# HGRN2's diagonal 32-position blocks as 32-column products, four column tiles to a product, into a compact tile

## The chip, the cores and the metric
One core of a Trainium2 chip runs the whole program. The metric is the device time of one execution in microseconds; a run's time stands as it was measured, and the profile is one further look at one execution, taken by the hardware profiler.

## The reference, cut to what matters
One inference step of a decoder layer: an input projection, two groups of four heads each (mLSTM and HGRN2), an output projection, and a SwiGLU feed-forward, for 1024 prompt tokens and 8 decode sequences of 4 tokens. The change is in HGRN2 alone, whose chunk is

```python
b = jnp.cumsum(lf, axis=2)
inter = jnp.einsum('bhtk,bhkv->bhtv', q * jnp.exp(b), S)
dec = jnp.exp(jnp.where(mask[:, :, None], b[:, :, :, None, :] - b[:, :, None, :, :], -jnp.inf))
A = jnp.einsum('bhtk,bhsk,bhtsk->bhts', q, k, dec)
o = inter + jnp.einsum('bhts,bhsv->bhtv', A, v)
```

The matrix A (position s, position t, with s not after t) has a decay for each feature between s and t. It must be right for every pair of positions in a chunk; how it is put together is free.

## The kernel before, in words
**Layout and stages.** Features lie on the 128 partitions, tokens along the free axis. The tokens come in three blocks of 288, 384 and 384 (the first holds 256 prompt tokens and the 32 decode tokens), that is 2, 3 and 3 chunks of 128 positions. First the input projection runs: 33 weight tiles, for each head four units per block (`unit`, L121, and `emit_k`, L124). A unit is one weight tile times one block: eight steps of three matmuls, the weights and the tokens being split into a high and a low part (L135, L136, L137). Then follow the output projection and the feed-forward, all in matmuls of 264 columns.

**What sets the order.** Every engine runs its instructions in the order in which the program emits them. Projection matmuls are emitted unit by unit; after every six of them `hook` (L63) is called, which gives each open generator a turn. `mix_b(h, b)` (L745) is such a generator, one for each head and block of HGRN2, twelve in all. `yield 2` means: go on at the second hook from here, so twelve projection matmuls lie between two parts. Weight splits (`split`, L86: ScalarE copies the high part, GpSimd subtracts) and the decode sequences (`sample_core`, L600) are generators too.

**How A is put together.** `mix_b` doubles a distance `lv` from 1 to 64. At each level it multiplies the keys with the queries on TensorE (`prod`, L754), then scales every second group of `lv` queries on VectorE (L801), the other groups of keys on GpSimd (L802), and makes the next level's gate products on VectorE (L806). The next product needs both. From each level's product only the entries belong to A in which s lies in an even group of `lv` positions and t in the odd group behind it; the diagonal comes from a product ahead of the levels. For the diagonal and levels 1 to 16 `prod` multiplies all 128 positions of a chunk with all 128 (L757), although only the four 32x32 blocks on the diagonal are read. The first block has, for the diagonal and levels 1 and 2, a further 32x32 product for the decode tokens (L759), which goes to the tile `PB`.

**From PSUM into the square tile `AT`** ([128, 3 chunks, 128]): for each of the four 32-row blocks one VectorE instruction. The diagonal is a product with the identity (L772), levels 1 to 8 are masked copies (L813, masks `mk`), level 16 is a plain copy of 16 rows (L821). Levels 32 and 64 have smaller products (L788: two column tiles of 32; L793) and are copied by ScalarE (L825, L827). Then keys and values are transposed (L840, L843), the state is brought forward (L857, L867), and `AT` and the state are multiplied with the values and queries (L877, L879).

Of the kernel before, what the change touches and what calls it, by code (L numbers as in the profile page):

```python
# [9 lines left out]
F32 = mybir.dt.float32  # L10
# [24 lines left out]
LEVELS = [1, 2, 4, 8]  # L35
# [5 lines left out]
def hybrid_step(ctx: ExitStack, tc: tile.TileContext, i, o):  # L41
# [109 lines left out]
    cst = mp.tile([128, 232], F32, name="cst")  # L151
    msk = mp.tile([128, 64], U8, name="msk")
# [28 lines left out]
    mk = {1: msk[:, 0:16], 2: msk[:, 16:32], 4: msk[:, 32:48], 8: msk[:, 48:64]}  # L181
# [16 lines left out]
    def norm_rstd(key, n, acc, w=(2, 3)):  # L198
        """the rstd of n tokens on all partitions, from the squares summed over the feature tiles in acc"""
        yield w[0]  # L200
        pc = bank()
        parts = [(t, min(128, n - 128 * t)) for t in range(3)]
        rs = cn.tile([128, 4], F32, tag="nrs", name="nrs", bufs=2)
        if parts[2][1] < 128:
            nc.vector.memset(rs, 1.0)
        for t, c in parts:
            nc.tensor.matmul(pc[:c, t:t + 1], acc[:, 128 * t:128 * t + c], ones, start=True, stop=True)
        for c, t0, t1 in [(128, 0, 3)] if n == 384 else [(128, 0, 2), (n - 256, 2, 3)]:
            nc.vector.tensor_scalar(rs[:c, t0:t1], pc[:c, t0:t1], 1.0 / D, EPS, op0=OP.mult, op1=OP.add)
        nc.gpsimd.tensor_tensor(rs[:, 0:3], rs[:, 0:3], mhalf[:, 0:3], op=OP.pow)  # L210
        done.add(("rs", key))
        yield w[1]
        pb = bank()
        for t, c in parts:
            nc.tensor.transpose(pb[:, 128 * t:128 * t + c], rs[:c, t:t + 1].to_broadcast([c, 128]), ident[:c, :c])
        return pb

    def norm_gen(key, x, hv, lv, acc, vg, w=(2, 3), pb=None, lo_dve=(0, 4), step=2):
        """x = hv + lv = x * rstd * g, rstd from the squares summed over the feature tiles in acc"""
        n = x.shape[2]  # L220
        if pb is None:
            pb = yield from norm_rstd(key, n, acc, w)

        def low(m):
            (nc.vector if m in lo_dve else nc.gpsimd).tensor_tensor(lv[:, m, :], x[:, m, :], hv[:, m, :].bitcast(F32),
                                                                    op=OP.subtract)
        for m in range(KT):
            nc.vector.scalar_tensor_tensor(x[:, m, :], x[:, m, :], col(vg + m), pb[:, :n], op0=OP.mult, op1=OP.mult)
            nc.scalar.activation(hv[:, m, :], x[:, m, :], AF.Copy)
            if m:  # L230
                low(m - 1)
            if m == KT - 1:
                low(m)
            if (m + 1) % step == 0:
                yield 1

    # ------------------------------------------------------------------ token mixers
# [3 lines left out]
    # per-feature constants  # L241
# [7 lines left out]
    def conv_consts():  # L249
        # half the convolution and half the output gate: y sigmoid(y) = (y/2) (tanh(y/2) + 1)  # L250
# [17 lines left out]
    # ---- mLSTM gates  # L268
# [84 lines left out]
    def gates_sample(ig, lf):  # L353
# [36 lines left out]
        for a in ATs:  # L390
            nc.gpsimd.memset(a, 0.0)
# [4 lines left out]
    # ---- mLSTM  # L396
# [93 lines left out]
    def norm_cols(s, sqs, nch, d2=None, p=128):  # L490
        """s = (sqs / 128 + EPS * d2) ** -0.5"""
# [108 lines left out]
    def sample_core(h_off, w, vnorm, st_in, decay, out_state, n_io, d2, k_scale, later=None):  # L600
        """the decode sequences of one head group: four heads x 32 tokens on the partitions"""
# [126 lines left out]
    # ---- HGRN2  # L728
    ATs = [mp.tile([128, 3, 128], F32, name=f"AT{j}") for j in range(2)]
    atn = [0]  # L730
# [14 lines left out]
    def mix_b(h, b):  # L745
        ncb, npr, n = NCH[b], NPR[b], BL[b]
        q, f, k = S["qb", h, b], S["f", h, b], S["kb", h, b]
        AT = ATs[atn[0] % 2]
# [5 lines left out]
        def prod(ps, a, c_, lo=0):  # L754
            for c in range(ncb):
                s = slice(c * 128, c * 128 + 128)
                nc.tensor.matmul(ps[:, s], a[:, s], c_[:, s], start=True, stop=True)  # L757
            if lo:
                nc.tensor.matmul(ps[32 * h:32 * h + 32, 256:288], a[:, 256:288], c_[:, 256:288], start=True, stop=True,  # L759
                                 tile_position=(0, 32 * h))  # L760

        def quads(fn):
            for j in range(4):
                fn(slice(32 * j, 32 * j + 32))
# [4 lines left out]
        prod(ps, k, q, samp)  # L769

        def dg(js):
            nc.vector.tensor_tensor(AT[js, :ncb, js], ps[js, :npr].rearrange("p (c t) -> p c t", t=128)[:, :, js],  # L772
                                    ident[js, None, js].to_broadcast([32, ncb, 32]), op=OP.mult)
        quads(dg)
        if samp:
            nc.vector.tensor_tensor(PB[hs, hs], ps[hs, 256:288], ident[hs, hs], op=OP.mult)
        yield 2
        G, go, lv = f, 0, 1
        while lv < 128:
# [3 lines left out]
            if lv <= 16:  # L783
                prod(ps, k, qp, sm)
# [23 lines left out]
            if lv <= 8:  # L808
                def ext(js):
                    src = pc[js, :, js].rearrange("p c (n two l) -> p c n two l", two=2, l=lv)[:, :, :, 1, :]  # L810
                    dst = AT[js, :ncb, js].rearrange("p c (n two l) -> p c n two l", two=2, l=lv)[:, :, :, 1, :]
                    m = mk[lv][js].rearrange("p (n l) -> p n l", l=lv)
                    nc.vector.copy_predicated(dst, m[:, None].to_broadcast([32, ncb, 16 // lv, lv]), src)  # L813
                quads(ext)
                if sm:
                    src = ps[hs, 256:288].rearrange("p (n two l) -> p n two l", two=2, l=lv)[:, :, 1, :]
                    dst = PB[hs, hs].rearrange("p (n two l) -> p n two l", two=2, l=lv)[:, :, 1, :]
                    nc.vector.copy_predicated(dst, mk[lv][hs].rearrange("p (n l) -> p n l", l=lv), src)
            elif lv == 16:
                for j in range(4):  # L820
                    nc.vector.tensor_copy(AT[32 * j:32 * j + 16, :ncb, 32 * j + 16:32 * j + 32],  # L821
                                          pc[32 * j:32 * j + 16, :, 32 * j + 16:32 * j + 32])
# [80 lines left out]
    # ------------------------------------------------------------------ unit list  # L903
# [37 lines left out]
    # output projection; the token order from here on: 1024 prompt tokens, 32 decode tokens  # L941
# [62 lines left out]
    # feed-forward, first NPLAIN feature tiles  # L1004
# [36 lines left out]
    # feed-forward, the other feature tiles: pairs of them (rows of A) times two halves of the tokens (columns of B), the  # L1041
    # contraction in two halves: the seven products of Strassen and Winograd
# [21 lines left out]
    def t_prep():  # L1064
        """T1 = B12 - B11, T2 = B22 - T1, T3 = B22 - B12, T4 = B21 - T2"""
# [71 lines left out]
    def gsplit(g, u, dve=False):  # L1137
        """the factors of the products: A11 A12 | S1 = A21 + A22, S2 = S1 - A11 | S3 = A11 - A21, A22 | S4 = A12 - S2"""
# [52 lines left out]
    def g_out(u, r, th, j, ps, other=None, op=None):  # L1191
        """row tile r, token half th, columns j: ps or ps + other is there"""
# [54 lines left out]
    # down projection: NS times four feature tiles in the same way (the contraction in two pairs of tiles, pairs of output  # L1247
    # tiles, halves of the tokens), the last two tiles plainly
# [3 lines left out]
    def memb(r):  # L1252
        """place r of the ring of operands: hi and lo of two feature tiles, half of the tokens"""
# [18 lines left out]
    def raw_ff(c, f):  # L1272
        """the two column blocks of a feature tile: halves of the tokens, in the last chunk halves of each half"""
# [16 lines left out]
    def stage1(c):  # L1290
        """B11, T1 = B12 - B11, T2 = B22 - T1, B21"""
# [26 lines left out]
    def diffs(c, k):  # L1318
        """T3 = B22 - B12, T4 = B21 - B11 - T3"""
# [7 lines left out]
    def stage2(c):  # L1327
        """B22, T3, T4"""
# [28 lines left out]
    def dsplit(g):  # L1357
        """A11 A12 A22 | S1 = A21 + A22, S2 = S1 - A11, S4 = A12 - S2, S3 = A11 - A21"""
# [5 lines left out]
        def pair(j):  # L1364
            # the weights of the last chunk stay: five tiles in the ring, three in free places of the other ring
# [49 lines left out]
    def d_step(g, p):  # L1415
        """a product for a pair of output tiles, halves of the tokens; in the last chunk for two pairs, the quarters of a half"""
# [27 lines left out]
    # the first NPLAIN feature tiles of the down projection plainly  # L1444
# [36 lines left out]
    # the final norm: the first half of the tokens, then two quarters  # L1481
    fac, frs = {}, {}

    def xs(m, q):
        """tile m for a half of the tokens (q = 0, 1) or quarter q = 2, 3"""
        return x2[0][:, m, 528 * q:528 * q + 528] if q < 2 else x2[0][:, m, q * QN:(q + 1) * QN]

    def fsquare(m, q, acc=None):
        """the squares of a tile, in a sum's first tile or for facc"""
# [5 lines left out]
    def facc(acc, sq, dve, wait=0):  # L1495
        """a generator: acc += sq"""
# [8 lines left out]
    def squares(h):  # L1505
        """the first four tiles, half h of the tokens"""
# [14 lines left out]
    def last_squares(m, q):  # L1521
        """the last four tiles of a quarter, as they are done"""
# [48 lines left out]
    def final_half():  # L1571
        """the first half of the tokens"""
# [20 lines left out]
    # ------------------------------------------------------------------ emission  # L1593
# [14 lines left out]
    nc.scalar.dma_start(cst, i["cst"][:, 128:360])  # L1608
# [62 lines left out]
    nc.vector.tensor_copy(msk, cst[:, 168:232])  # L1671
# [165 lines left out]
def _constants():  # L1837
    p = np.arange(128)
    cst = np.zeros((128, 360), np.float32)
# [5 lines left out]
    msk = cst[:, 296:360]  # L1845
    r = p % 32
    for j, l in enumerate(LEVELS):
        n = np.arange(16) // l
        msk[:, 16 * j:16 * j + 16] = ((r[:, None] // (2 * l)) == n[None, :]) & ((r[:, None] % (2 * l)) < l)
    return cst  # L1850
# [63 lines left out]
```

## Time and profile before

| | |
|---|---|
| three runs | 1456.2, 1456.57, 1451.91 us (median 1456.2) |
| profiled execution | span 1451.2 us; the page gives no other time of its own |
| TensorE | 1376.6 us busy (95%), 10384 matmuls |
| VectorE | 904.0 us (62%), 2120 instructions |
| ScalarE | 528.8 us (36%) |
| GpSimd | 731.9 us (50%) |
| mean granted TensorE clock | 0.980 |

The span runs from the first to the last instruction of one execution. PE is TensorE's matmul, PEld its weight load, DVE is VectorE, ACT ScalarE, POOL GpSimd, SP SyncE. A line such as L757 is a line of the kernel. Matmul records overlap: one lasts longer than the distance to the next, so the time that a matmul takes from the stream is read from starts.

### The profile page before, as it was taken

The numbers are of one execution on the slowest core, as the hardware profiler recorded it, in microseconds if no ns is written. First come the engines' busy times: TensorE is split into PE (matmuls) and PEld (weight loads), VectorE is DVE, ScalarE is ACT, GpSimd is POOL, SyncE is SP. The second block draws the span as 40 slices with busy tenths as digits, with TensorE's granted clock in tenths as the row PEclk, the third lists the DMA queues.
The fourth block names the chain that finished last, engine by engine and source line by source line (L and its number), as shares of the span: only waits on it lengthen the run. The fifth ranks groups of instructions, "written<-read, shape, count | busy, mean of one in ns | idle before, by whom it ended". The sixth has DMA issues, their size and how long they took to land. (4 is left out here: it accounts for less than half of the span.)

```text
span 1451.2 us, 26916 instructions
## 1 busy us (share of the span) xinstructions
PE 1376.6 (95%) x10384; PEld 1339.6 (92%) x10384; DVE 904.0 (62%) x2120; ACT 528.8 (36%) x1195; POOL 731.9 (50%) x720
## 2 busy tenths in 40 slices
PE   7879999999999999999989999999999999998886
PEld 7769999999999998899989999999999998888885
DVE  7876657666776767745472233233322389999986
ACT  6554433322222223223344343333334423333343
POOL 5313213234343435223456655656555778888854
PEclk9989999999999999999999999999999999999998
DMA  6012212320010114443542222222212563334303
GB/s 216 22 42 76 64 37 86 109 79 29 33 44 18 44 32 133 142 148 119 182 139 74 82 89 89 69 72 89 89 64 69 182 235 134 134 134 145 123 30 121
DMA packets 85833, 138.54 MB, mean 95 GB/s; under 512 B 8240, under 2 KB 61000, under 8 KB 85192
## 3 DMA queue, kind: packets, MB, share of 16 engines
q1 hardware_dynamic: 85272, 136.57, 28.7%
q8 instruction: 82, 1.34, 0.4%
q14 instruction: 47, 0.39, 0.1%
q10 hardware_dynamic: 432, 0.24, 0.1%
HBM read 107.03 MB, written 29.75 MB: 94 GB/s over the span
## 5 line engine op out<-in xcount | busy, mean ns | idle before, releaser
L135 PE MATMUL mm<-HI,whi 128*128 128x384 f32 (+2 forms) x1160 | 382.7, 330 | 6.9 <-ACT gA L302 2.9
L137 PE MATMUL mm<-HI,wlo 128*128 128x384 f32 (+2 forms) x1160 | 363.8, 314 | 1.3 <-POOL wlo L97 1.3
L136 PE MATMUL mm<-LO,whi 128*128 128x384 f32 (+2 forms) x1160 | 363.9, 314 | 0.7 <-DVE LO L961 0.4
L135 PEld LDWEIGHTS mm<-HI,whi 128*128 128x128 f32 x1160 | 222.2, 192 | 12.2 <-ACT gA L302 3.2
L136 PEld LDWEIGHTS mm<-LO,whi 128*128 128x128 f32 x1160 | 222.4, 192 | 1.7 <-DVE LO L961 0.6
L137 PEld LDWEIGHTS mm<-HI,wlo 128*128 128x128 f32 x1160 | 221.9, 191 | 1.8 <-POOL wlo L97 1.8
L97 POOL TENSOR_TENSOR wlo<-raw,whi 128x512 fp32r<-128x512 f32 x90 | 119.7, 1339 | 144.1 <-ACT whi L96 99.2
L1158 POOL TENSOR_TENSOR wlo<-S,whi 128x512 fp32r<-128x512 f32 x78 | 107.0, 1373 | 87.1 <-ACT whi L1157 85.8
L1229 PE MATMUL mx<-T,whi 128*128 128x264 f32 x640 | 118.2, 284 | 0.0
L1229 PEld LDWEIGHTS mx<-T,whi 128*128 128x128 f32 x640 | 99.0, 188 | 0.0
L802 POOL TENSOR_TENSOR ck<-ck,wib 128x192 f32<-128x192 f32 (+2 forms) x72 | 41.2, 572 | 100.6 <-PE mx L757 56.2
L1229 PE MATMUL mx<-HI,whi 128*128 128x264 f32 x320 | 91.0, 284 | 0.0
L1229 PE MATMUL mx<-T,wlo 128*128 128x264 f32 x320 | 90.9, 284 | 0.0
L1229 PE MATMUL mx<-HI,wlo 128*128 128x264 f32 x320 | 90.9, 284 | 0.0
L1229 PE MATMUL mx<-LO,whi 128*128 128x264 f32 x320 | 90.7, 283 | 0.0
L1282 POOL TENSOR_TENSOR LO<-rg,HI 128x528 fp32r<-128x528 f32 x52 | 78.4, 1514 | 10.5 <-ACT HI L1281 5.8
L1435 PE MATMUL mx<-HI,whi 128*128 128x264 f32 x208 | 62.3, 300 | 9.9 <-DVE X L1439 9.9
L1157 ACT ACTIVATE whi<-S 128x512 fp32r<-128x512 f32 x80 | 50.2, 629 | 58.4 <-DVE S L1146 58.4
L1229 PE MATMUL mm<-HI,wlo 128*128 128x264 f32 x240 | 68.2, 284 | 0.0
L1229 PE MATMUL mm<-HI,whi 128*128 128x264 f32 x240 | 68.2, 284 | 0.0
L1229 PE MATMUL mm<-LO,whi 128*128 128x264 f32 x240 | 67.9, 283 | 0.0
L1439 DVE TENSOR_TENSOR X<-X,mx 128x264 f32<-128x264 f32 x160 | 60.7, 418 | 8.2 <-PE mx L1435 8.2
(544 smaller groups left out, 3751.8 us busy)
## 6 DMA issues: line engine op xcount, KB each, us to landing
rg<-d_ff SPq DMA_DIRECT2D x42, 528.0 KB
raw<-in_wA SPq DMA_DIRECT2D x31, 512.0 KB
raw<-in_wgu SPq DMA_DIRECT2D x24, 512.0 KB
raw<-in_wd SPq DMA_DIRECT2D x22, 512.0 KB
d_ff<-sg SPq DMA_DIRECT2D x40, 264.0 KB
rg<-in_wgu SPq DMA_DIRECT2D x20, 512.0 KB
d_h<-X SPq DMA_DIRECT2D x4, 1056.0 KB
X<-d_x SPq DMA_DIRECT2D x4, 1056.0 KB
```

The costliest lines, as they stand in the source:

```text
L97: (nc.gpsimd if pool else nc.vector).tensor_tensor(lo[:, s], raw[:, s], hi[:, s].bitcast(F32), op=OP.subtract)
L135: nc.tensor.matmul(ps[:, :n], wh, rh[:, k, :], start=(k == 0), stop=False)
L136: nc.tensor.matmul(ps[:, :n], wh, rl[:, k, :], start=False, stop=False)
L137: nc.tensor.matmul(ps[:, :n], wl, rh[:, k, :], start=False, stop=(k == nk - 1))
L802: nc.gpsimd.tensor_tensor(ke, ke, gv[:, :, 1:2].to_broadcast([128, nb, lv]), op=OP.mult)
L1157: nc.scalar.activation(hi[:, s], t, AF.Copy)
L1158: (nc.vector if dve else nc.gpsimd).tensor_tensor(lo[:, s], t, hi[:, s].bitcast(F32), op=OP.subtract)
L1229: nc.tensor.matmul(ps[:, :QN], a[:, w], b_[:, kk, c], start=new and kk == 0 and x == 0, stop=kk == 3 and x == 2, skip_group_check=True)
L1282: (nc.vector if dve else nc.gpsimd).tensor_tensor(lw, src, h.bitcast(F32), op=OP.subtract)
L1435: nc.tensor.matmul(ps[:, :QN], a[:, w], b_[k][:, cs], start=new and k == 0 and x == 0, stop=k == 1 and x == 2, skip_group_check=True)
L1439: nc.vector.tensor_tensor(y, y, ps[:, :QN], op=OP.add)
```

## The change
`prod` makes, for the diagonal and levels 1 to 16, one matmul for each 32-position block of a chunk: the 32 keys as weights in column tile j, 32 queries as moving columns for the diagonal, and for a level only the 16 queries that belong to odd groups. The products land compactly, on partitions 32j to 32j + 31 and 32 or 16 columns for each chunk. A compact tile `AD` ([128, 3, 32]) takes them by one masked copy over all 128 partitions at each level, with an identity mask for the diagonal and a new mask for level 16. After level 16 ScalarE copies the four blocks of `AD` into the diagonal blocks of `AT`. The decode product of the first block uses the same code (column tile h). The constants grow from 232 to 296 columns, two `AD` tiles are cleared with the `AT` tiles, and the descriptor scratch gets a size of 2048 bytes a partition. Comments and docstrings go.

```diff
-LEVELS = [1, 2, 4, 8]
+LEVELS = [1, 2, 4, 8, 16]
-    cst = mp.tile([128, 232], F32, name="cst")
-    msk = mp.tile([128, 64], U8, name="msk")
+    cst = mp.tile([128, 296], F32, name="cst")
+    msk = mp.tile([128, 128], U8, name="msk")
-        for a in ATs:
+        for a in ATs + ADs:
             nc.gpsimd.memset(a, 0.0)
+    ADs = [mp.tile([128, 3, 32], F32, name=f"AD{j}") for j in range(2)]
-        def prod(ps, a, c_, lo=0):
-            for c in range(ncb):
-                s = slice(c * 128, c * 128 + 128)
-                nc.tensor.matmul(ps[:, s], a[:, s], c_[:, s], start=True, stop=True)
-            if lo:
-                nc.tensor.matmul(ps[32 * h:32 * h + 32, 256:288], a[:, 256:288], c_[:, 256:288], start=True, stop=True,
-                                 tile_position=(0, 32 * h))
+        def prod(ps, a, c_, lv, lo=0):
+            w = 16 if lv else 32
+            for c in range(ncb + (1 if lo else 0)):
+                for j in range(4) if c < ncb else (h,):
+                    s0 = c * 128 + 32 * j if c < ncb else 256
+                    rhs = c_[:, s0:s0 + 32]
+                    dst = ps[32 * j:32 * j + 32, c * w:c * w + w]
+                    if lv:
+                        rhs = rhs.rearrange("p (n two l) -> p n two l", two=2, l=lv)[:, :, 1, :]
+                        dst = dst.rearrange("p (n l) -> p n l", l=lv)
+                    nc.tensor.matmul(dst, a[:, s0:s0 + 32], rhs, start=True, stop=True, tile_position=(0, 32 * j))
...
-        def dg(js):
-            nc.vector.tensor_tensor(AT[js, :ncb, js], ps[js, :npr].rearrange("p (c t) -> p c t", t=128)[:, :, js],
-                                    ident[js, None, js].to_broadcast([32, ncb, 32]), op=OP.mult)
-        quads(dg)
+        nc.vector.copy_predicated(AD[:, :ncb, :], mk[0][:, None].to_broadcast([128, ncb, 32]),
+                                  ps[:, :32 * ncb].rearrange("p (c t) -> p c t", t=32))
...
-            if lv <= 8:
-                def ext(js):
-                    src = pc[js, :, js].rearrange("p c (n two l) -> p c n two l", two=2, l=lv)[:, :, :, 1, :]
-                    dst = AT[js, :ncb, js].rearrange("p c (n two l) -> p c n two l", two=2, l=lv)[:, :, :, 1, :]
-                    m = mk[lv][js].rearrange("p (n l) -> p n l", l=lv)
-                    nc.vector.copy_predicated(dst, m[:, None].to_broadcast([32, ncb, 16 // lv, lv]), src)
-                quads(ext)
+            if lv <= 16:
+                src = ps[:, :16 * ncb].rearrange("p (c n l) -> p c n l", c=ncb, l=lv)
+                dst = AD[:, :ncb, :].rearrange("p c (n two l) -> p c n two l", two=2, l=lv)[:, :, :, 1, :]
+                m = mk[lv].rearrange("p (n l) -> p n l", l=lv)
+                nc.vector.copy_predicated(dst, m[:, None].to_broadcast([128, ncb, 16 // lv, lv]), src)
...
-            elif lv == 16:
-                for j in range(4):
-                    nc.vector.tensor_copy(AT[32 * j:32 * j + 16, :ncb, 32 * j + 16:32 * j + 32],
-                                          pc[32 * j:32 * j + 16, :, 32 * j + 16:32 * j + 32])
+                if lv == 16:
+                    for j in range(4):
+                        js = slice(32 * j, 32 * j + 32)
+                        nc.scalar.activation(AT[js, :ncb, js], AD[js, :ncb, :], AF.Copy)
-    nc.scalar.dma_start(cst, i["cst"][:, 128:360])
+    nc.scalar.dma_start(cst, i["cst"][:, 128:424])
-    nc = _bacc.Bacc("TRN2", target_bir_lowering=False, num_devices=1)
+    nc = _bacc.Bacc("TRN2", target_bir_lowering=False, num_devices=1, dynamic_dma_scratch_size=2048)
```

## Rows read from the trace of the kernel before
**Rows 1.** The page: the span, and TensorE's busy time with its share.
```profile
span 1451.2 us, 26916 instructions
...
PE 1376.6 (95%) x10384; PEld 1339.6 (92%) x10384; DVE 904.0 (62%) x2120; ACT 528.8 (36%) x1195; POOL 731.9 (50%) x720
```
**Rows 2.** Windows: stretch, its length, each engine's busy us (instructions), clock, DMA share, GB/s.
```profile
308.00:600.00 292.00, 287.41 (x2129) 273.54 (x2128) 213.64 (x666) 81.04 (x218) 118.72 (x165) 0.99 0.18 55
600.00:1300.00 700.00, 683.64 (x5486) 677.34 (x5485) 344.78 (x642) 253.51 (x541) 414.47 (x336) 0.99 0.35 115
```
**Rows 3.** Lines by form, 308 to 600: the 128-column products; busy us, mean ns.
```profile
L757 PE MATMUL mx<-qw,ck 128*128 128x128 f32 x320 | 45.5, 275 | 0.6 <-POOL ck L802 0.4 <-DVE wib L806 0.2
...
L757 PE MATMUL mx<-cq,ck 128*128 128x128 f32 x64 | 9.1, 275 | 0.0
```
**Rows 4.** Timeline of TensorE, a three-chunk product: start us, us, instruction.
```profile
332.06 0.34 PE L137 MATMUL mm<-HI,wlo 128*128 128x384 f32 x1
332.23 0.83 PE L757 MATMUL mx<-qw,ck 128*128 128x128 f32 x6
...
333.07 0.34 PE L136 MATMUL mm<-LO,whi 128*128 128x384 f32 x1
```
**Rows 5.** Timeline of TensorE, the level-32 product of three chunks.
```profile
346.95 0.34 PE L137 MATMUL mm<-HI,wlo 128*128 128x384 f32 x1
347.22 0.38 PE L788 MATMUL mx<-qw,ck 128*32 128x32 f32 x12
...
347.81 0.34 PE L136 MATMUL mm<-LO,whi 128*128 128x384 f32 x1
```
**Rows 6.** Timeline of TensorE, two-chunk products, with the decode chunk and without it.
```profile
312.95 0.29 PE L137 MATMUL mm<-HI,wlo 128*128 128x288 f32 x1
313.08 0.61 PE L757 MATMUL mx<-qw,ck 128*128 128x128 f32 x4
313.62 0.25 PE L759 MATMUL mx<-qw,ck 128*32 128x32 f32 x2
...
314.04 0.29 PE L136 MATMUL mm<-LO,whi 128*128 128x288 f32 x1
...
315.68 0.30 PE L137 MATMUL mm<-HI,wlo 128*128 128x288 f32 x1
315.81 0.61 PE L757 MATMUL mx<-qw,ck 128*128 128x128 f32 x4
...
316.43 0.34 PE L136 MATMUL mm<-LO,whi 128*128 128x384 f32 x1
```
**Rows 7.** A decode product in four column tiles: in the timeline, and its line.
```profile
554.22 0.43 PE L672 MATMUL so<-st,qz 128*32 128x128 f32 x8
...
L672 PE MATMUL so<-st,qz 128*32 128x128 f32 x64 | 3.6, 301 | 0.4 <-POOL qz L633 0.4
```
**Rows 8.** Lines by form, 308 to 600: VectorE's copies into the square tile.
```profile
L813 DVE COPY_PREDICATED AT<-msk,mx 32x48 f32<-32x48 uint8 x128 | 29.7, 232 | 3.2
...
L813 DVE COPY_PREDICATED AT<-msk,mx 32x32 f32<-32x32 uint8 x64 | 13.1, 205 | 1.5
...
L772 DVE TENSOR_TENSOR AT<-mx,ident 32x96 f32<-32x96 f32 x32 | 8.1, 254 | 12.6 <-PE mx L757 11.9
...
L821 DVE COPY AT<-mx 16x48 f32<-16x48 f32 x32 | 6.5, 202 | 0.8
```
**Rows 9.** Waits of TensorE, 308 to 610: us in total, times, longest.
```profile
PE mx L788 <- DVE wib L806: 2.0, 1, 2.0
PE mx L793 <- POOL ck L802: 1.0, 1, 1.0
```
**Rows 10.** Weight loads after the longest of these waits, and the window behind it.
```profile
557.84 0.32 PEld L788 LDWEIGHTS mx<-qw,ck 128*32 128x32 f32 x12 [2.26 <-POOL wlo L97]
...
558.10:561.50 3.40, 3.40 (x24) 2.52 (x19) 3.31 (x10) 2.18 (x5) 1.94 (x4) 0.50 0.25 63
```
**Rows 11.** Lines by form, 308 to 600: ScalarE's copies of level 32.
```profile
L825 ACT ACTIVATE AT<-mx 32x96 f32<-32x96 f32 x16 | 3.9, 241 | 13.0 <-PE mx L788 12.9
```

More of the change, by code (lines that the diff above doesn't have):

```diff
@@ L180, in hybrid_step @@
     maskneg, seqm, mneg4 = cst[:, 0:128], cst[:, 128:136], cst[:, 136:168]
-    mk = {1: msk[:, 0:16], 2: msk[:, 16:32], 4: msk[:, 32:48], 8: msk[:, 48:64]}
+    mk = {1: msk[:, 0:16], 2: msk[:, 16:32], 4: msk[:, 32:48], 8: msk[:, 48:64], 16: msk[:, 64:80], 0: msk[:, 96:128]}
     nc.scalar.preload_act_table_set("sqrt_and_others")
@@ L747, in mix_b @@
         q, f, k = S["qb", h, b], S["f", h, b], S["kb", h, b]
-        AT = ATs[atn[0] % 2]
+        AT, AD = ATs[atn[0] % 2], ADs[atn[0] % 2]
         atn[0] += 1
@@ L752, in mix_b @@
         qp = tl("qw")
-        def prod(ps, a, c_, lo=0):
-            for c in range(ncb):
-                s = slice(c * 128, c * 128 + 128)
-                nc.tensor.matmul(ps[:, s], a[:, s], c_[:, s], start=True, stop=True)
-            if lo:
-                nc.tensor.matmul(ps[32 * h:32 * h + 32, 256:288], a[:, 256:288], c_[:, 256:288], start=True, stop=True,
-                                 tile_position=(0, 32 * h))
-        def quads(fn):
-            for j in range(4):
-                fn(slice(32 * j, 32 * j + 32))
+        def prod(ps, a, c_, lv, lo=0):
[9 more added lines that the diff above has]
+                    nc.tensor.matmul(dst, a[:, s0:s0 + 32], rhs, start=True, stop=True, tile_position=(0, 32 * j))
         hs = slice(32 * h, 32 * h + 32)
@@ L768, in mix_b @@
         ps = bank()
-        prod(ps, k, q, samp)
-        def dg(js):
-            nc.vector.tensor_tensor(AT[js, :ncb, js], ps[js, :npr].rearrange("p (c t) -> p c t", t=128)[:, :, js],
-                                    ident[js, None, js].to_broadcast([32, ncb, 32]), op=OP.mult)
-        quads(dg)
+        prod(ps, k, q, 0, samp)
+        nc.vector.copy_predicated(AD[:, :ncb, :], mk[0][:, None].to_broadcast([128, ncb, 32]),
+                                  ps[:, :32 * ncb].rearrange("p (c t) -> p c t", t=32))
         if samp:
-            nc.vector.tensor_tensor(PB[hs, hs], ps[hs, 256:288], ident[hs, hs], op=OP.mult)
+            nc.vector.tensor_tensor(PB[hs, hs], ps[hs, 64:96], ident[hs, hs], op=OP.mult)
         yield 2
@@ L783, in mix_b @@
             if lv <= 16:
-                prod(ps, k, qp, sm)
+                prod(ps, k, qp, lv, sm)
             elif lv == 32:
@@ L807, in mix_b @@
             pc = ps[:, :npr].rearrange("p (c t) -> p c t", t=128)
-            if lv <= 8:
-                def ext(js):
-                    src = pc[js, :, js].rearrange("p c (n two l) -> p c n two l", two=2, l=lv)[:, :, :, 1, :]
-                    dst = AT[js, :ncb, js].rearrange("p c (n two l) -> p c n two l", two=2, l=lv)[:, :, :, 1, :]
-                    m = mk[lv][js].rearrange("p (n l) -> p n l", l=lv)
-                    nc.vector.copy_predicated(dst, m[:, None].to_broadcast([32, ncb, 16 // lv, lv]), src)
-                quads(ext)
+            if lv <= 16:
[3 more added lines that the diff above has]
+                nc.vector.copy_predicated(dst, m[:, None].to_broadcast([128, ncb, 16 // lv, lv]), src)
                 if sm:
-                    src = ps[hs, 256:288].rearrange("p (n two l) -> p n two l", two=2, l=lv)[:, :, 1, :]
+                    src = ps[hs, 32:48].rearrange("p (n l) -> p n l", l=lv)
                     dst = PB[hs, hs].rearrange("p (n two l) -> p n two l", two=2, l=lv)[:, :, 1, :]
                     nc.vector.copy_predicated(dst, mk[lv][hs].rearrange("p (n l) -> p n l", l=lv), src)
-            elif lv == 16:
-                for j in range(4):
-                    nc.vector.tensor_copy(AT[32 * j:32 * j + 16, :ncb, 32 * j + 16:32 * j + 32],
-                                          pc[32 * j:32 * j + 16, :, 32 * j + 16:32 * j + 32])
+                if lv == 16:
+                    for j in range(4):
+                        js = slice(32 * j, 32 * j + 32)
+                        nc.scalar.activation(AT[js, :ncb, js], AD[js, :ncb, :], AF.Copy)
             elif lv == 32:
@@ L1670, in hybrid_step @@
     hook()
-    nc.vector.tensor_copy(msk, cst[:, 168:232])
+    nc.vector.tensor_copy(msk, cst[:, 168:296])
     nxt = 2
@@ L1838, in _constants @@
     p = np.arange(128)
-    cst = np.zeros((128, 360), np.float32)
+    cst = np.zeros((128, 424), np.float32)
     cst[:, 0:128] = np.eye(128)
@@ L1844, in _constants @@
     cst[:, 264:296] = np.where((s // 4 == t // 4) & (s <= t), 0.0, -1e30)
-    msk = cst[:, 296:360]
+    msk = cst[:, 296:424]
     r = p % 32
@@ L1849, in _constants @@
         msk[:, 16 * j:16 * j + 16] = ((r[:, None] // (2 * l)) == n[None, :]) & ((r[:, None] % (2 * l)) < l)
+    msk[:, 96:128] = r[:, None] == np.arange(32)[None, :]
     return cst
```

## The prediction
> **What bounds the kernel now.** The page comes first: TensorE is busy 95% of a span of 1451.2 us [rows 1]. Then the windows, because 95% is a mean over stages. In the stretch in which HGRN2's blocks run, 308 to 600 us, TensorE is busy 287.4 of 292.0 us, VectorE 213.6, ScalarE 81.0, GpSimd 118.7; after it, from 600 to 1300 us, TensorE is busy 683.6 of 700.0 us [rows 2]. So in the changed stage a microsecond that leaves TensorE's stream is a microsecond off the end, unless a wait grows in its place; and behind it nothing but TensorE's own stream sets the pace, so that what is gained arrives at the end. A busy TensorE says nothing on how long one product holds it up, since records overlap. That I read from starts in the timeline: from the last projection matmul ahead of a product to the second one behind it, less the two steps that these matmuls take without it. Last come the lines of VectorE (what is merged) and the waits of TensorE (what a lighter VectorE could give back).
>
> **TensorE, what a product costs before.** The f32 products issue two instructions per 128-column matmul: 320 + 64 = 384 records [rows 3] are 32 chunks (two for each of four first blocks, three for each of eight others) times six products times two. A step of a 384-column projection matmul is 0.17 us, of a 288-column one 0.13 us [rows 4, 6].
> - Three chunks: 333.07 - 332.06 = 1.01 us, less 2 x 0.17: 0.67 us [rows 4]. There are 8 x 6 = 48.
> - Two chunks with the decode chunk: 314.04 - 312.95 = 1.09, less 2 x 0.13: 0.83 us [rows 6]. There are 4 x 3 = 12 (diagonal, levels 1 and 2).
> - Two chunks alone: 316.43 - 315.68 = 0.75, less 0.13 + 0.17: 0.45 us [rows 6]. There are 4 x 3 = 12 (levels 4, 8, 16).
>
> **What it costs after.** No product of four column tiles with 16 or 32 moving columns stands in this trace, but two neighbours do. The level-32 product has two column tiles and 32 columns: twelve instructions cost 347.81 - 346.95 - 2 x 0.17 = 0.52 us, and they last 0.38 us from the first start to the last end while one lasts about 0.20, so that the starts spread over some 0.18 us [rows 5]. Two tiles run beside each other: that is six rounds of about 0.03 us, and some 0.33 us is left that does not grow with the count (entering and leaving the column layout). The decode product has four column tiles and 128 columns: eight instructions last 0.43 us at a mean of 0.30 us for one [rows 7]. Eight instructions of 128 columns one after another would spread over 7 x 0.11 us (the 0.67 us over six instructions); they spread over 0.13 to 0.16, so four tiles do run beside each other.
>
> A new three-chunk product is 12 matmuls, 24 instructions, four to a round: again six rounds of 0.03 us, plus 0.02 us for the three more starts in the last round: 0.53 us. Two chunks are four rounds: 0.48 us; with the decode chunk six, the last two on one tile: 0.53 us. Ends: if the 16-column products are bound by starts alone (0.007 us each, four starts within 0.02 us in [rows 7]), 0.50 us; if nothing overlaps, 24 x 0.03 + 0.33 = 1.05 us. I take 0.53, because it is nearest to the level-32 row, which has the same moving width and weights.
>
> The Trainium skill speaks against this step: "TensorEngine Tiling (Array Packing)", section "Instruction Overhead", gives every matmul an overhead of about 60 cycles, however few its columns, and advises against tiling by a dimension that is already small. An estimate from that page, with 60 cycles at 2.4 GHz as 25 ns one after another, is 24 x 0.025 + 0.33 = 0.93 us a product. Here the trace disagrees for two tiles: twelve in some 0.18 us are about 16 ns each [rows 5]; for four tiles of 16 columns no run shows it yet.
>
> Sum on TensorE: 48 x (0.53 - 0.67) = -6.7; 12 x (0.53 - 0.83) = -3.6; 12 x (0.48 - 0.45) = +0.4. Together -9.9 us. Ends: at 0.50 us for a product -2 more, -12; with no overlap 48 x 0.38 + 12 x (18 x 0.03 + 0.33 - 0.83 = 0.04) + 12 x (16 x 0.03 + 0.33 - 0.45 = 0.36) = +23.
>
> **VectorE.** Before, a three-chunk block spends 4 x 254 (diagonal) + 16 x 232 (levels 1 to 8) + 4 x 202 ns (level 16) = 5.5 us on copies over 32 or 16 partitions [rows 8]. After, each level is one masked copy over 128 partitions with the same 48 elements in each: 5 x 232 ns. The diagonal has 96 elements; from 32 to 48 elements the time grows by 27 ns (205 to 232), so 232 + 3 x 27 = 313 ns. That is 1.5 us, 4.1 less; a two-chunk block saves some 3.5. Over the stage 8 x 4.1 + 4 x 3.5 = 47 of 213.6 us. VectorE is not the bound, so most of it is worth nothing. It is worth something where TensorE waited on a late VectorE queue: 2.0 us in front of the level-32 product for VectorE's gate products and 1.0 us on keys that GpSimd scaled late, behind a norm that VectorE delivered late [rows 9]; after the first the granted clock was 0.50 for 3.4 us, 1.7 us lost [rows 10]. In front of each of the two waits a group of four copies leaves the queue (0.92 to 0.23 us, four times 232 ns against one): 0.7 each, 1.4 us, and I add 0.6 for some of the half clock. So -2.0; ends 0 (other work sets the queue) and -4.7 (2.0 + 1.0 + 1.7).
>
> **ScalarE.** It gains four copies per block from the compact tile into the square one, 48 in all; by the nearest row, 32x96 at 241 ns [rows 11], 11.6 us on an engine busy 81 of 292. Each first one waits for the level-16 masked copy and stands in order before projection evictions and weight splits. Three projection banks cover it: a unit of 24 matmuls takes 24 x 0.17 = 4.2 us, so an eviction may be two units late before TensorE stops. The matmul that reads the square tile comes after two more levels and six further hooks. Cost 0; without the cover, the four copies in each of 12 blocks, 11.6 us.
>
> **The rest.** The constants' transfer is 64 columns longer, the mask copy is one VectorE instruction as before, and GpSimd clears two more small tiles: +0.2 us, about one small VectorE copy [rows 8], 0 to 0.5. No transfer is moved past another, and the size of the descriptor scratch issues no instruction: 0.
>
> **Sum:** -9.9 - 2.0 + 0.2 = -11.7 us: span 1451.2 to 1439.5. For the profiled execution the page gives no time beside its span; that lies 5.0 us under the median of the runs, 1456.2, and 0.7 under their lowest, 1451.91. The change is taken off the median: 1444.5 us.
>
> **Rivals.**
> 1. Only two tiles run beside each other. Then 24 instructions are twelve rounds: 12 x 0.03 + 0.33 = 0.69 us. 48 x 0.02 + 12 x (9 x 0.03 + 0.33 - 0.83 = -0.23) + 12 x (8 x 0.03 + 0.33 - 0.45 = 0.12) = -0.4; with VectorE's part -2.2: 1454, no change. For it: [rows 5]; against: [rows 7].
> 2. The time goes into waits: scaled keys or queries come late and TensorE stands as long as before, 1456. For it: [rows 9]. Against: they start when a product ends, and the twelve projection matmuls (2.07 us) in front of the next stay.
> 3. Nothing overlaps, because 16-column instructions are bound by their own start or weight load: +23 - 1.8 = +21: 1477, slower. It decides from 14 ns a start ((0.67 - 0.33) / 24); the level-32 row stands at 16 with two tiles, [rows 7] under it only in bursts of four. By the skill's overhead it would be 48 x 0.26 + 12 x (-0.05) + 12 x 0.28 = +15 us, an estimate.
> 4. TensorE's instruction feed falls behind, also slower. A period gets 36 matmuls and as many weight loads, 72 instructions in 2.07 + 0.53 = 2.6 us, 36 ns each, where projections of 384 columns need one per 85 ns. The slowest feed that the rows allow is one per 65 ns (a 288-column step of 0.13 us is a load and a matmul [rows 6]); a period would take 4.7 us, and 72 products at +2.1 are up to 150 us: about 1600 at worst. It decides from some 40 ns on. Against: when the 2.0 us wait ended, twelve loads and matmuls of the level-32 product started within 0.3 us [rows 10], some 10 ns each; they may have been queued already. The Trainium skill, "TensorE: Matmul & The Clock Gate", section "Wait — 56ns, not 53.3ns?", puts a matmul at about 62 ns when the sequencer's microcode decodes it. If that counted matmuls alone, 36 would take 2.2 us, an estimate, and fit; no row here tells which decoding is on.
>
> **How the numbers follow.** Forecast 0.78; rival 1 0.06; rival 2 0.06; rival 3 0.06; rival 4 0.04. A change under 0.3% (4.4 us) cannot be told from none. Faster is the forecast and a sliver of rival 1, 0.79; same is the rest of rivals 1 and 2, 0.11; slower is 3 and 4, 0.10. Low end 1436: -12 on TensorE and -4.7 on waits is 1439.7, and up to 4 lower if the runs lie where the lowest one did. High end 1455 takes in rivals 1 and 2 in the main.
>
> **What would show it.** Right: product starts in bursts of four, 0.53 us by the same reading for 24 instructions; masked copies of 128x48 near 232 ns; VectorE under 170 us in the stage; a stage about 11 us shorter; no wait on the square tile. Wrong: starts 30 ns apart (rival 3), gaps in the projection matmuls behind a product with no named releaser (rival 4), or a wait on the scaled keys after every product (rival 2).

## The result and the profile after

| | before | changed |
|---|---|---|
| median of 5 runs | 1455.05 us (1451.91 to 1456.57) | 1445.84 us (1442.07 to 1447.60) |
| ratio to before | | 0.9938, 95% interval 0.9923 to 0.9954 |
| span of the profiled execution | 1451.2 us | 1443.4 us (its time 1445.25) |
| TensorE, matmuls | 1376.6 us, 10384 | 1364.6 us, 11536 |
| VectorE, instructions | 904.0 us, 2120 | 845.2 us, 1904 |
| ScalarE, instructions | 528.8 us, 1195 | 542.3 us, 1243 |

The change is faster by 9.2 us (by the ratio's interval 6.7 to 11.2). Forecast were 11.7 us less and a time of 1444.5. The sum is 2.5 us off: one of its terms, put at 0, cost about 5 us, and products that gave a little more than forecast hide part of it. The time is nearer (1.3 us) than the sum, because the median that was taken for the kernel before, 1456.2, lay 1.2 us above the one of five runs.

The same stretches as in [rows 2], of the kernel after (columns as there):

```profile
308.00:600.00 292.00, 284.16 (x3339) 256.51 (x3338) 159.49 (x463) 95.73 (x274) 119.29 (x167) 0.99 0.19 57
600.00:1300.00 700.00, 683.17 (x5485) 676.31 (x5484) 350.35 (x648) 256.04 (x541) 420.20 (x340) 0.99 0.35 116
```

VectorE fell from 213.6 to 159.5 us in the changed stage, ScalarE rose from 81.0 to 95.7. TensorE is still busy 97% there, but a little less than before (284.2 against 287.4 us): it waits more. The next stage stands as it was.

The products in TensorE's timeline, of the kernel after: three chunks (answers to [rows 4]), two with the decode chunk, two alone (both to [rows 6]):

```profile
356.24 0.34 PE L137 MATMUL mm<-HI,wlo 128*128 128x384 f32 x1
356.51 0.38 PE L767 MATMUL mx<-qw,ck 128*32 128x16 f32 x24
...
357.11 0.34 PE L136 MATMUL mm<-LO,whi 128*128 128x384 f32 x1
...
311.96 0.29 PE L137 MATMUL mm<-HI,wlo 128*128 128x288 f32 x1
312.18 0.36 PE L767 MATMUL mx<-qw,ck 128*32 128x16 f32 x18
...
312.71 0.29 PE L136 MATMUL mm<-LO,whi 128*128 128x288 f32 x1
...
316.45 0.29 PE L137 MATMUL mm<-HI,wlo 128*128 128x288 f32 x1
316.67 0.32 PE L767 MATMUL mx<-qw,ck 128*32 128x16 f32 x16
...
317.19 0.34 PE L136 MATMUL mm<-LO,whi 128*128 128x384 f32 x1
```

Read as before: 357.11 - 356.24 - 0.35 = 0.52 us; 0.75 - 0.26 = 0.49; 0.74 - 0.30 = 0.44. (Two steps of a 384-column matmul are 0.347 us by the starts ahead of the product; the prediction took 0.34. The distance averaged over the 24 three-chunk products that stand between 384-column matmuls is 1.018 us in the trace of before and 0.864 in this one: 0.67 and 0.52 less the same 0.347.) The 24 instructions of the first last 0.38 us, as long as the twelve of the level-32 product with two column tiles [rows 5]: four tiles beside each other cost what two did. By these prices TensorE's part is 48 x (0.52 - 0.67) + 12 x (0.49 - 0.83) + 12 x (0.44 - 0.45) = -11.4 us.

The diagonal's product has 32 moving columns instead of 16, and its 24 instructions last 0.40 us (TensorE's timeline, of the kernel after):

```profile
353.88 0.40 PE L767 MATMUL mx<-cq,ck 128*32 128x32 f32 x24
```

So half the moving columns saved next to nothing; what counts here is how many rounds of column tiles a product has.

VectorE's masked copies, by line in the stage, of the kernel after; they answer to [rows 8]:

```profile
L812 DVE COPY_PREDICATED AD<-msk,mx 128x48 f32<-128x48 uint8 x40 | 8.8, 219 | 0.0
...
L773 DVE COPY_PREDICATED AD<-msk,mx 128x96 f32<-128x96 uint8 x8 | 2.1, 269 | 10.0 <-PE mx L767 10.0
```

Over 128 partitions one takes 219 ns, no more than over 32 (232 forecast), and the diagonal's 269 (313 forecast).

The waits of TensorE in the stage (engine, line, whom it waited for: us in total, times, longest), of the kernel after; they answer to [rows 9]:

```profile
PE mx L793 <- POOL ck L802: 4.2, 4, 2.4
PE mx L793 <- DVE wib L806: 2.0, 1, 2.0
...
PE mx L788 <- DVE wib L806: 0.5, 1, 0.5
```

In front of the level-64 product (L793) TensorE now stands 6.2 us in five waits; it was 1.0 us in one. The wait in front of level 32 fell from 2.0 to 0.5, by more than the 0.7 us forecast for it. So the gain of the products arrives less what these five waits take. What they wait for shows in ScalarE's and GpSimd's timelines, first of the kernel before:

```profile
345.56 0.63 ACT L96 ACTIVATE whi<-raw 128x512 fp32r<-128x512 f32 x1
...
346.27 1.45 POOL L97 TENSOR_TENSOR wlo<-raw,whi 128x512 fp32r<-128x512 f32 x1 [0.18 <-ACT whi L96]
347.92 0.51 POOL L802 TENSOR_TENSOR ck<-ck,wib 128x192 f32<-128x192 f32 x1 [0.20 <-DVE AT L821]
```

and at the same place of the kernel after:

```profile
344.97 0.57 ACT L742 ACTIVATE ck<-mm,nbf 128x384 f32<-128x384 f32 x1
346.50 1.16 ACT L820 ACTIVATE AT<-AD 32x96 f32<-32x96 f32 x4 [0.96 <-DVE AD L812]
347.68 0.63 ACT L96 ACTIVATE whi<-raw 128x512 fp32r<-128x512 f32 x1
...
348.39 1.29 POOL L97 TENSOR_TENSOR wlo<-raw,whi 128x512 fp32r<-128x512 f32 x1 [2.99 <-ACT whi L96]
349.64 0.51 POOL L802 TENSOR_TENSOR ck<-ck,wib 128x192 f32<-128x192 f32 x1
...
350.21 0.56 PE L793 MATMUL mx<-qw,ck 128*64 128x64 f32 x6 [0.60 <-POOL ck L802]
```

Before, ScalarE split a weight tile at 345.56, GpSimd subtracted in 346.27 to 347.72, and was free for the key scaling of level 32. After, ScalarE ends its last eviction at 345.54, stands 0.96 us for VectorE's level-16 copy, makes the four copies in 1.16 us, and only then comes to the split. GpSimd idles 2.99 us and then does the subtraction ahead of the key scaling, in the order in which they were emitted. The keys are ready at 350.15, and the level-64 product starts 0.6 us late.

One difference between the two profiles is none of the change's. TensorE waits 1.6 us near 252 us in both, long before the first product. In the window behind it the granted clock is 1.00 (2.4 GHz) in the kernel before and 0.50 (1.2 GHz) in the kernel after (third column from the end). By half of these 3.4 us that is an estimated 1.7 us of the profiled execution, and the first product does start 1.8 us later:

```profile
253.70:257.10 3.40, 3.40 (x21) 3.40 (x20) 2.60 (x10) 1.40 (x7) 0.19 (x1) 1.00 0.36 133
```

```profile
253.70:257.10 3.40, 3.40 (x13) 3.40 (x13) 2.68 (x10) 1.10 (x6) 0.11 (x1) 0.50 0.45 155
```

Behind the two longest of the five waits, which end at 554.4 and 584.5 us, the granted clock of the kernel after is 0.50 too:

```profile
554.10:557.50 3.40, 3.13 (x14) 2.92 (x14) 3.40 (x6) 1.53 (x4) 3.10 (x6) 0.50 0.85 255
584.80:588.20 3.40, 3.40 (x18) 3.28 (x17) 2.08 (x8) 0.50 (x2) 0.63 (x1) 0.50 0.95 253
```

The kernel before has one such stretch, behind its wait of 2.0 us [rows 10]. Such a stretch does not follow every time: of the experiments below, the repeat has it behind the second of these waits alone, and the kernel before with the copies added, which waits 2.1 and 2.3 us there, behind neither (granted clock 1.00 from 308 to 610 us).

From the first product to the first matmul of the feed-forward's seven-product part it is 437.8 us before (308.3 to 746.1) and 428.5 us after (310.1 to 738.6): 9.3 less, as the medians say; the spans differ by 7.8.

### The profile page after: what moved, and what is told of

It reads as the page before. It is cut to its first block, busy times and chain, and to the rows that moved or that the text cites. A ratio compares the mean times of both kernels' runs of the same rounds, so it can differ in the third digit from the quotient of the medians.

```text
span 1443.4 us, 29053 instructions
## 1 busy us (share of the span) xinstructions
PE 1364.6 (95%) x11536; PEld 1313.5 (91%) x11536; DVE 845.2 (59%) x1904; ACT 542.3 (38%) x1243; POOL 730.4 (51%) x722
## 5 line engine op out<-in xcount | busy, mean ns | idle before, releaser
L135 PEld LDWEIGHTS mm<-HI,whi 128*128 128x128 f32 x1160 | 221.7, 191 | 11.5 <-ACT gA L302 3.2
```

The source lines that it names most:

```text
L135: nc.tensor.matmul(ps[:, :n], wh, rh[:, k, :], start=(k == 0), stop=False)
```

## The experiments

Theory A: ScalarE's four copies behind level 16 stand in a queue that runs in order; what is behind them comes late and ends as a wait at level 64. Theory B: TensorE's sooner arrival makes the waits, whoever copies. Each set of runs has its own runs of before, and ratios are to those.

**The changed kernel again,** beside the next three.

> The changed kernel once more, beside the others on one chip. Both theories: 6 to 11 us faster than before; product of 24 instructions 0.52 us between its neighbours, five waits in front of the level-64 product (three of 0.6 to 0.8 us, two of 2.0 to 2.4 us). What differs from the first profile by itself is the half-clock stretches, which may fall elsewhere.

Measured: 1445.65 us, 0.9946 (0.9928 to 0.9964). The same five waits, again 4.2 and 2.0 us; the profile's span, 1444.4 us, is near the first one's.

**The copies on VectorE.**

```diff
-                        nc.scalar.activation(AT[js, :ncb, js], AD[js, :ncb, :], AF.Copy)
+                        nc.vector.tensor_copy(AT[js, :ncb, js], AD[js, :ncb, :])
```

> The four copies from the compact into the square tile go to VectorE instead of ScalarE, all else as changed. Theory A (ScalarE's copies stand in its queue until VectorE's level-16 copy is done, so weight splits and high parts behind them are late, then GpSimd's key scaling or VectorE's gate products, then TensorE at level 64): the three waits of 0.6 to 0.8 us vanish, the two of about 2 us fall under 1.2 us, and the time falls by 3 to 6 us against the changed kernel, to 12 to 15 us below before. Theory B (TensorE now reaches level 64 sooner than GpSimd and VectorE can be ready, whoever copies): the waits in front of level 64 stay at 6 to 7 us in total and the time is that of the changed kernel within 1.5 us.

Measured: 1442.65 us, 0.9932 (0.9917 to 0.9948), which overlaps the interval of the changed kernel. Theory A's forecast of the waits failed: the three short ones stayed, with another releaser. Theory B's failed too: the waits sum to 5.3 us, where it had 6 to 7, and the time is 3.0 us under the changed kernel's by the medians, where it had at most 1.5. TensorE's waits of this kernel:

```profile
PE mx L793 <- DVE wib L806: 3.9, 4, 2.0
PE mx L793 <- POOL ck L802: 1.4, 1, 1.4
```

Its VectorE and GpSimd around one of them:

```profile
348.45 1.01 DVE L820 COPY AT<-AD 32x96 f32<-32x96 f32 x4
349.50 1.44 DVE L801 TENSOR_TENSOR qw<-qw,wib 128x192 f32<-128x192 f32 x1
350.86 0.15 DVE L806 TENSOR_TENSOR wib<-wib 128x6 f32<-128x6 f32 x1
...
349.44 1.28 POOL L97 TENSOR_TENSOR wlo<-raw,whi 128x512 fp32r<-128x512 f32 x1 [0.46 <-ACT whi L96]
```

ScalarE and GpSimd are on time again. But now VectorE's query scaling (L801) stands behind the copies, starts 0.06 us after a subtraction of GpSimd and takes 1.44 us instead of 0.36. So copies in the place behind level 16 delay what stands behind them on either engine; "ScalarE's queue" alone was too narrow.

**The copies on ScalarE, later.** The four lines go from level 16 to where the state is brought forward, two hooks (twelve projection matmuls) ahead of the matmul that reads them.

```diff
-                if lv == 16:
-                    for j in range(4):
-                        js = slice(32 * j, 32 * j + 32)
-                        nc.scalar.activation(AT[js, :ncb, js], AD[js, :ncb, :], AF.Copy)
...
+        for j in range(4):
+            js = slice(32 * j, 32 * j + 32)
+            nc.scalar.activation(AT[js, :ncb, js], AD[js, :ncb, :], AF.Copy)
         prev = Sst.get(h)
```

> The same four ScalarE copies, emitted after the state's matmul instead of after level 16, where VectorE's copy has long been done. Theory A: no wait for VectorE in front of them, the waits in front of the level-64 product sum to under 2.5 us instead of 7, and the time is 3 to 7 us below the changed kernel. Theory B: waits and time as in the changed kernel. If ScalarE's 1.16 us a block itself is the harm and not where it stands, the waits move to the matmul behind the copies.

Measured: 1439.55 us, 0.9902 (0.9888 to 0.9917), clear of the changed kernel's interval: 6.1 us less by the medians. Its copies, by line: the idle time in front of 32 of them is 0.3 us, where it was 12.9. First this kernel, then the changed one:

```profile
L855 ACT ACTIVATE AT<-AD 32x96 f32<-32x96 f32 x32 | 8.9, 278 | 0.3
```

```profile
L820 ACT ACTIVATE AT<-AD 32x96 f32<-32x96 f32 x32 | 9.0, 281 | 12.9 <-DVE AD L812 12.6
```

Of the waits at level 64 one of 0.3 us is left. Two waits for decode states show that the changed kernel did not have, and one of 0.2 us for the copies themselves (waits of TensorE, this kernel):

```profile
PE so L672 <- DMA st<-in_S: 2.3, 2, 1.2
...
PE mx L793 <- POOL ck L802: 0.3, 1, 0.3
...
PE mx L874 <- ACT AT L855: 0.2, 1, 0.2
```

The copies take as long as before (278 against 281 ns) and cost 0.2 us of waiting where nothing near is due. Theory B is out: TensorE arrives just as soon here, and does not wait.

**Four masked copies a level again,** into the compact tile, ScalarE's copies as in the changed kernel.

```diff
+                for j in range(4):
+                    js = slice(32 * j, 32 * j + 32)
...
-                nc.vector.copy_predicated(dst, m[:, None].to_broadcast([128, ncb, 16 // lv, lv]), src)
+                    nc.vector.copy_predicated(dst, m[:, None].to_broadcast([32, ncb, 16 // lv, lv]), src)
```

> The new products stay, but each masked copy is made as four of 32 partitions again (VectorE as loaded as before, plus nothing). If VectorE's relief is worth the 2 us of the forecast (or more, since the waits at level 64 run over VectorE): 2 to 5 us slower than the changed kernel. If the change's gain is TensorE's products alone: the changed kernel's time within 1.5 us. Product cost 0.52 us either way; VectorE busy about 45 us more.

Measured: 1447.67 us, 0.9960 (0.9947 to 0.9973); VectorE 210.3 us in the stage against 159.5. By the medians 2.0 us slower than the changed kernel beside it, but the intervals overlap. The wait in front of level 32 came back in part (1.1 us in two waits against 0.5 in one). A second pair of runs points the same way: the kernel with late copies has the relief, the one with the new products alone (below) has not, and by the ratios the first is 3.5 us faster, with intervals that overlap again. VectorE's relief is worth about what was forecast or a little more, if anything; these runs do not settle it.

**The products' order.** The same matmuls, all chunks of a tile one after another.

```diff
-            for c in range(ncb + (1 if lo else 0)):
-                for j in range(4) if c < ncb else (h,):
+            order = [(c, j) for j in range(4) for c in range(ncb)] + ([(ncb, h)] if lo else [])
+            for c, j in order:
+                if True:
```

> The same matmuls, emitted tile by tile (all chunks of column tile 0, then of tile 1, and so on) instead of chunk by chunk. If four tiles overlap only because neighbours in the stream go to different tiles (rival 3 of the prediction is then what the order has avoided): starts 0.03 us apart, a product of 24 instructions 0.9 to 1.1 us, the kernel 25 to 40 us slower than the changed one and slower than before. If TensorE picks ready matmuls from its queue whatever their order: 0.52 us and the time of the changed kernel within 2 us.

Measured: 1455.78 us, 1.0013 (1.0003 to 1.0023): the whole gain is gone, and neither number was met. A three-chunk product of this kernel in TensorE's timeline:

```profile
346.15 0.34 PE L137 MATMUL mm<-HI,wlo 128*128 128x384 f32 x1
346.42 0.63 PE L768 MATMUL mx<-qw,ck 128*32 128x16 f32 x24
...
347.26 0.34 PE L136 MATMUL mm<-LO,whi 128*128 128x384 f32 x1
```

It costs 1.11 - 0.35 = 0.76 us: the same 24 instructions last 0.63 us instead of 0.38, a start each 19 ns instead of 8 (0.63 or 0.38 less 0.19 for one, over 23). Some overlap stays: the last three starts of such a product in the trace, with one tile left to go, lie 31 to 32 ns apart. 48 x 0.24 = 11.5 us, and 9.7 were lost against the changed kernel by the ratios. With two chunks, four instructions in a row on a tile instead of six, the order costs almost nothing (TensorE's timeline, the changed kernel first, then this one):

```profile
450.82 0.32 PE L767 MATMUL mx<-qw,ck 128*32 128x16 f32 x16
```

```profile
457.57 0.34 PE L768 MATMUL mx<-qw,ck 128*32 128x16 f32 x16
```

So the overlap of four tiles hangs on neighbours in the stream going to different tiles when six instructions in a row go to one; with four in a row 0.02 us was lost. Why the step lies between these two stays open.

**The kernel before, with ScalarE's copies added,** into a spare tile that nobody reads. This kernel also has the changed one's size of the descriptor scratch.

```diff
+                for j in range(4):
+                    js = slice(32 * j, 32 * j + 32)
+                    nc.scalar.activation(AD[js, :ncb, :], AT[js, :ncb, js], AF.Copy)
```

> The kernel before, with one thing of the change added: four ScalarE copies per block behind level 16, from the square tile into a spare one that nobody reads. Theory A (the copies' place in ScalarE's queue): TensorE gets waits in front of the level-64 product (it has one of 1.0 us before), 3 to 6 us in total, and the kernel is 2 to 6 us slower than before. Theory B (only the sooner arrival of TensorE makes the waits): no new waits, the time of before within 1.5 us.

Measured: 1457.86 us, 1.0032 (1.0020 to 1.0045), some 4.7 us slower than before by the ratio. The waits of this kernel in front of level 64 (here L794):

```profile
PE mx L794 <- POOL ck L803: 4.4, 4, 2.3
PE mx L794 <- DVE wib L807: 2.1, 1, 2.1
```

That is 6.5 us in five waits, a little more than expected, with the old products and their old arrival. The copies make them without the new products.

**The new products alone,** into the square tile by four masked copies at every level, 16 too, and nothing on ScalarE.

```diff
-                    dst = AD[js, :ncb, :].rearrange("p c (n two l) -> p c n two l", two=2, l=lv)[:, :, :, 1, :]
+                    dst = AT[js, :ncb, js].rearrange("p c (n two l) -> p c n two l", two=2, l=lv)[:, :, :, 1, :]
```

(this line against the kernel with four masked copies; the diagonal's copy goes to `AT` in the same way, and the ScalarE copies are gone)

> The new products alone: every level, 16 too, goes from its compact PSUM columns straight into the square tile by four masked copies of 32 partitions, so there are no compact tile, no ScalarE copies and no relief of VectorE. Theory A: TensorE's 11 us remain and the waits are those of before (7 us in the stage), so 9 to 12 us below before, that is 0 to 3 us below the changed kernel. Theory B: waits at level 64 of 5 us or more, as in the changed kernel, and a time of 1446 or more.

Measured: 1441.85 us, 0.9926 (0.9909 to 0.9943): 10.8 us by the ratio, with the waits of before (here L795 is level 64 and L790 level 32), VectorE at 215.2 us. TensorE's term, -11.4 by the prices above, arrives nearly whole. The waits of this kernel:

```profile
PE mx L790 <- DVE wib L808: 2.0, 2, 1.8
PE mx L795 <- POOL ck L804: 1.1, 1, 1.1
```

**A third buffer for the decode states,** on top of the late copies, fetched three ahead.

```diff
-            st = mp.tile([128, 4, 130], F32, tag="st", name="st", bufs=2)
+            st = mp.tile([128, 4, 130], F32, tag="st", name="st", bufs=3)
...
+        fetch(2)
...
-            if s + 2 < SEQS:
-                fetch(s + 2)
+            if s + 3 < SEQS:
+                fetch(s + 3)
             yield 3 if later is None else 2
```

> The kernel with late ScalarE copies, and a third buffer for the decode states, fetched three ahead, against the 2.3 us that TensorE waited there for a state's transfer (two waits of 1.2 and 1.1 us). If those waits are on the path: they vanish and the time falls by 1 to 3 us below the late-copy kernel (1437 to 1439). If something else is late right behind (the output projection's high and low parts on ScalarE and VectorE): waits move there, and the time stays within 1 us.

Measured: 1438.30 us, 0.9894 (0.9880 to 0.9909). The waits for states are gone from TensorE's list and nothing took their place. By the medians it is 1.3 us below the late-copy kernel, by ratios to their own runs of before 0.0008; the intervals overlap. Both kernels beat the changed one clearly; between the two the time does not decide.

## Why the prediction was right, and where it was not

- **TensorE's term held:** -9.9 forecast, -11.4 by the new prices, 10.8 with the products alone. A three-chunk product was 0.52 us for 0.53. With two chunks it was 0.49 for 0.53 and 0.44 for 0.48: sixteen starts spread over 0.32 - 0.19 = 0.13 us, the four rounds that were counted, so it is the entering and leaving that came out shorter. The neighbours in the trace of before (two tiles of the same width, four tiles of a greater width) were enough to price an operation that it did not have.
- **Rivals 1 and 3 are out for the order as written.** Rival 3's mechanism is real in part all the same: by tiles instead of chunks the three-chunk products lose so much of the overlap that the whole gain is gone. The overhead of about 60 cycles for each matmul, which the Trainium skill gives in "TensorEngine Tiling (Array Packing)", section "Instruction Overhead", would be 25 ns at 2.4 GHz, an estimate. With four tiles taking turns the trace disagrees with it: measured are 8 ns a start, and some 17 ns for a matmul, which is two instructions here. Tile by tile it is 19 ns a start, 38 ns a matmul, which does not contradict it.
- **Rival 4 is out.** A period's 72 instructions run in 2.07 + 0.52 us, and the second matmul behind a product comes 0.29 us after the first (356.82 to 357.11), as it did behind the level-32 product before (0.28, 347.53 to 347.81).
- **The step that failed is ScalarE's: "Cost 0".** I named the cover for evictions (three projection banks) and it held. I did not price the weight splits and high parts that stand in the same queue, although the prediction named the splits as queued behind. Behind a split stands GpSimd's subtraction, behind it GpSimd's key scaling, behind it the next product. The first copy waits 0.96 us and the four take 1.16, which moved the next split from right behind the last eviction to 2.1 us after it. The price is 4.7 us added to the kernel before, 6.1 us taken out of the changed one; the end that I gave without cover, 11.6 us, was too far.
- **VectorE's term, -2.0, was right at one place and covered at the other.** The wait in front of level 32 fell from 2.0 to 0.5 us. The wait at level 64 did not fall, because it now came by way of ScalarE. Rival 2 named just that (late scaled keys) and was half true: five waits, where I argued that the twelve projection matmuls cover them. They cover one subtraction of 1.3 us in front of the key scaling if it starts on time, and not if it starts 2.1 us late.

As a sum: -11.4 (products), -2.0 to -3.5 (VectorE, not settled), +4.7 to +6.1 (copies): -7.3 to -10.2, against 9.2 measured and 7.8 by the ratio of the repeat. That the forecast of 11.7 came within 2.5 us of the measured change is in part luck: its largest term was sound, and the cost that it left out was half hidden by products that came out cheaper and perhaps by VectorE.

## What to carry to other kernels

Price a new operation by its nearest neighbours in the trace, and count it by rounds of column tiles. Emit consecutive matmuls to different tiles: here six instructions in a row on one tile lost 0.24 us a product, four in a row 0.02. When copies are moved to an idle engine, ask not how busy that engine is but what stands behind them in its queue and who waits for that; an instruction that waits for another engine belongs where nothing behind it is due. A copy whose reader comes much later can go to a later place almost for nothing.

## What the runs showed of the hardware

A VectorE instruction that started beside a GpSimd subtraction of 1.28 us took 1.44 us, where the same instruction took 0.36 us in the kernel with late copies, with GpSimd at a scaling of 0.67 us beside it. That kernel, on VectorE:

```profile
347.39 0.36 DVE L801 TENSOR_TENSOR qw<-qw,wib 128x192 f32<-128x192 f32 x1
```

In the kernel with the copies on VectorE (its rows stand above) it ran from 349.50 to 350.94 and the subtraction from 349.44 to 350.72. It ended 0.22 us after the subtraction. The kernel before has a case of the same kind: the subtraction at 346.27 ended at 347.72, and VectorE's gate product, begun 0.23 us behind its start, ended at 347.75:

```profile
346.50 1.25 DVE L806 TENSOR_TENSOR wib<-wib 128x12 f32<-128x12 f32 x1
```

In the changed kernel, with GpSimd idle, the same instruction took 0.17 us (at 346.18). Masked copies, which read their product from PSUM, were not held: in the trace of the changed kernel those of 128x48 that began 0.07 or 0.26 us into such a subtraction took 0.25 us. So work that is late on GpSimd can hold VectorE too; why was not tested here.

The granted clock after the same wait of 1.6 us was 1.00 in one profile and 0.50 for 3.4 us in the other, so an estimated 1.7 us of a profile can be chance.
